# Weight subtractions of three attention stages on VectorE instead of GpSimd, and the value product emitted ahead of normalising q and k

## The chip, the cores and the metric

The kernel runs on one core of a Trainium2 chip. The metric is the time of one execution on the device, in microseconds (us); of several runs the median is taken.

A core has five engines, each with its own instruction queue that it works off in order: TensorE (PE, matrix products; PEld is its weight load), VectorE (DVE), ScalarE (ACT), GpSimd (POOL) and SyncE (SP), which issues the weight transfers here. An instruction that waits for another engine holds up all that stands behind it in its own queue.

## The reference

One sequence of 256 tokens with 1024 features goes through two transformer blocks of two layers with a mixture of experts, and then four layers with a plain MLP. The mixers, in order, are forgetting attention, latent attention, retention, block attention with a relative bias ("moba"), differential attention ("diff") and retention again. Cut to the two mixers that the change touches most:

```
# moba; 256 tokens are one block of 256, so every query sees its own causal block alone
q, k, v = split(h @ w_in, 3)                       # 16 heads of 64
q = rmsnorm(q, q_norm_w) * 64 ** -0.5;  k = rmsnorm(k, k_norm_w)
p = softmax(where(dist >= 0, q @ k.T + bias[bucket(dist)], -1e30))
out = (p @ v) @ w_out

# diff; 16 heads of q and k, 8 of v with 128 columns
p = softmax(as above).reshape(8 heads, 2, q, k)
o = (p[:, 0] - lambda * p[:, 1]) @ v
out = (rmsnorm(o, subln_w) * (1 - lambda_init)) @ w_out
```

Latent attention projects h to 768 columns for queries and a shared 256+32 for keys and values, and expands these per head; the rest of it is attention again.

## The kernel before

All weights are float32 in device memory. To multiply with them nearly exactly, the kernel makes two numbers of each: `wh`, the weight rounded to the engine's fast format, and `wl = raw - wh`, what the rounding lost. Activations are split in the same way (`hTh`, `hTl`; `aTh`, `aTl`). A product of such a pair is three matmuls: high by high, high by low, low by high (L169 to L171 in `tok_mm` with 256 columns each, and likewise in `feat_mm` and `acc_mm`).

`unit` (L137 to L156) brings in one weight block: SyncE starts the transfer into `raw`, ScalarE casts to `wh` (L147), and `wl` is made by one subtraction per piece of 128x1024 (or smaller) (L153). Which engine makes that subtraction is read from the table `SPL` by the name of the stage: with (1, 0) every subtraction of the stage is GpSimd's, with (2, 0) every second, and a stage that isn't in the table has them on VectorE. Before the change five stages are in it: forgetting attention (`fgt`), the two halves of latent attention (`latpre`, `latheads`), `moba` and `diff`. GpSimd makes 127 subtractions in all, 34 in `fgt`, 10 in `latpre`, 15 in `latheads`, 34 in `moba` and 34 in `diff`; VectorE makes 399 in the other stages and in half of `latheads`.

`_attn_layer` is the program of `moba` and of `diff`. It works on four groups of four heads. For a group, `proj` (L635 to L672) loads the weights of q, k and v (`uq`, `uk`, `uv`, two pieces each), multiplies h with q's and k's for both halves of the tokens (96 matmuls), squares the result on ScalarE (L647), adds it up by head on VectorE (L648, L652), takes the inverse root (`rsqrt`, L253 to L263, some twelve tiny VectorE operations on 128x16), scales q and k with it on VectorE (L659), transposes them on TensorE (L663) and copies them out on ScalarE. Only then comes the product with v's weights (L667 to L671, 48 matmuls). `mix` does the attention: scores on TensorE (L523), bias and row maximum on VectorE (L531), its sign (L533), exponential on ScalarE (L535), transposing the probabilities (L545) and the product with v. In `diff`, VectorE combines the two softmaxes (L690 to L693), and after the product ScalarE squares the result (L704), VectorE takes the inverse root again (L706, L253 to L263, here on 128x2 and 128x1) and scales (L710), and TensorE transposes the result (L210).

The order on each engine is set by a scheduler that goes by the order in which the code emits the work and by the engines' expected times, so work of the next group (its q and k products, tiles `pj__...`) is put between the dependent steps of the present one. `HOLD` sets from which subtraction on a stage's subtractions may not be placed ahead of a given point; it isn't changed.

Of the kernel before, what the change touches and what calls it, by code (L numbers as in the profile page):

```python
# [10 lines left out]
F32 = mybir.dt.float32  # L11
# [10 lines left out]
NT = S // 128  # L22
# [8 lines left out]
GU = 2  # L31
GE = 4
HOLD = dict(ret0=2, mlp0=2, mlp1=2, mlp2=2, mlp3=2, moba=4)
SPL = {'fgt': (1, 0), 'latpre': (1, 0), 'latheads': (2, 0), 'moba': (1, 0), 'diff': (1, 0)}
HL = 6
WX = 2
HOMES = "rhrhxhrhrhxhr"
# [47 lines left out]
class Net:  # L85
# [51 lines left out]
    def unit(self, ap, k, n):  # L137
# [4 lines left out]
        for k0 in range(0, k, step):  # L142
# [5 lines left out]
            self.nu += 1  # L148
            sh = SPL.get(self.ph, ())
            eng = nc.gpsimd if sh and self.nu % sh[0] in sh[1:] else nc.vector  # L150
# [462 lines left out]
    def _attn_layer(self, i, kind):  # L613
        nc, I = self.nc, self.I
        diff = kind == "diff"
        w, wo = I[kind + "_w_in_2"][0], I[kind + "_w_out_2"][0]
        gq = self.head_gain(I[kind + "_q_norm_2"][0], 0.125)
        gk = self.head_gain(I[kind + "_k_norm_2"][0], 1.0)
        if diff:
            init = 0.8 - 0.6 * math.exp(-0.3 * i)  # L620
            lb = self.bcast_row(I["diff_lambda_2"][0], 256, tag="lam")
            lv = lb.rearrange("p (a b d) -> p a b d", a=2, b=2)
            pr = self.wk.tile([128, 2, 64], F32, name="lpr", tag="lam")
            nc.vector.tensor_tensor(pr, lv[:, :, 0, :], lv[:, :, 1, :], OP.mult)
            l2 = self.sm.tile([128, 2], F32, name="l2", tag="l2")
            nc.vector.tensor_reduce(l2, pr, AX.X, OP.add)
            nc.scalar.activation(l2, l2, AF.Exp)
            nlam = self.sm.tile([128, 1], F32, name="nlam", tag="nlam")
            nc.vector.tensor_tensor(nlam, l2[:, 1:2], l2[:, 0:1], OP.subtract)
            nc.vector.tensor_scalar(nlam, nlam, -init, None, op0=OP.add)  # L630
            sub = self.bcast_row(I["diff_subln_2"][0], 128, tag="sub")
            nc.vector.tensor_scalar(sub, sub, 1.0 - init, None, op0=OP.mult)
        hT, r = self.prenorm(self.column("norm1_2", i * D))

        def proj(g):  # L635
            uq = self.unit(self.rows(w, 0, 8, g * 256, 256), 8, 256)
            uk = self.unit(self.rows(w, 0, 8, 1024 + g * 256, 256), 8, 256)
            uv = self.unit(self.rows(w, 0, 8, 2048 + g * 256, 256), 8, 256)
            bias = self.load_bias(g)
            ss = self.sm.tile([128, NT, 8], F32, name="qss", tag="qss")  # L640
            pss = []
            for tok in range(NT):
                ps = self.ppj()
                self.tok_mm(ps[:, 0:256], hT, tok, uq, 8, 0, True, True)
                self.tok_mm(ps[:, 256:512], hT, tok, uk, 8, 0, True, True)
                sq = self.wk.tile([128, 512], F32, name="sq", tag="sq")
                nc.scalar.activation(sq, ps, AF.Square, scale=r[:, tok:tok + 1])  # L647
                nc.vector.tensor_reduce(ss[:, tok, :], sq.rearrange("p (h d) -> p h d", d=64), AX.X, OP.add)  # L648
                qk = self.wk.tile([128, 512], F32, name="qk", tag="qk", bufs=4)
                nc.scalar.copy(qk, ps)  # L650
                pss.append(qk)
            nc.vector.tensor_scalar(ss, ss, 1.0 / 64, EPS, op0=OP.mult, op1=OP.add)  # L652
            rr = self.rsqrt(ss.rearrange("p t h -> p (t h)"), 16).rearrange("p (t h) -> p t h", t=NT)
            qT = self.wk.tile([128, 2, S], F32, name="qT", tag="qT", bufs=3)
            kT = self.wk.tile([128, 2, S], F32, name="kT", tag="kT", bufs=3)
            for tok in range(NT):
                nc.vector.tensor_scalar(rr[:, tok, :], rr[:, tok, :], r[:, tok:tok + 1], None, op0=OP.mult)
                qk = pss[tok].rearrange("p (h d) -> p h d", d=64)
                nc.vector.tensor_tensor(qk, qk, rr[:, tok, :, None].to_broadcast([128, 8, 64]), OP.mult)  # L659
                pt = self.pat()  # L660
                pv = pt.rearrange("p (k t) -> p k t", k=4)
                for m in range(4):
                    nc.tensor.transpose(pv[:, m, :], pss[tok][:, m * 128:m * 128 + 128], self.ident)  # L663
                t = slice(tok * 128, tok * 128 + 128)
                nc.scalar.mul(qT[:, :, t], pv[:, 0:2, :], gq)
                nc.scalar.mul(kT[:, :, t], pv[:, 2:4, :], gk)
            v = self.wk.tile([128, NT, 256], F32, name="v", tag="v", bufs=3)  # L667
            ps = self.ppj()
            for tok in range(NT):
                self.tok_mm(ps[:, tok * 256:tok * 256 + 256], hT, tok, uv, 8, 0, True, True)  # L670
                nc.scalar.mul(v[:, tok], ps[:, tok * 256:tok * 256 + 256], r[:, tok:tok + 1])  # L671
            return qT, kT, v, bias  # L672

        def mix(g, aT, qT, kT, v, bias):

            def q(h):
                return qT[h % 2 * 64:h % 2 * 64 + 64, h // 2, :]

            def k(h):
                return kT[h % 2 * 64:h % 2 * 64 + 64, h // 2, :]  # L680

            def bq(h, qb):
                return bias[:, h, 128 - qb * 128:256]

            for qb in range(NT):
                nb = qb + 1
                if diff:
                    o = self.wk.tile([128, 256], F32, name="o", tag="o")
                    p, rs = self.probs(q, k, bq, qb)
                    nc.vector.tensor_scalar(rs[:, :, 1], rs[:, :, 1], nlam, None, op0=OP.mult)  # L690
                    for m in range(2):
                        nc.vector.tensor_scalar(p[0][:, m, :], p[0][:, m, :], rs[:, m, 0:1], None, op0=OP.mult)
                        nc.vector.scalar_tensor_tensor(p[0][:, m, :], p[1][:, m, :], rs[:, m, 1:2], p[0][:, m, :],  # L693
                                                       op0=OP.mult, op1=OP.add)
                    pT = self.flip([p[0][:, m, kb * 128:kb * 128 + 128] for m in range(2) for kb in range(nb)])
                    po = self.pat()
                    for dh in range(2):
                        for kb in range(nb):
                            nc.tensor.matmul(po[:, dh * 128:dh * 128 + 128], pT[dh * nb + kb],
                                             v[:, kb, dh * 128:dh * 128 + 128], start=kb == 0, stop=kb == nb - 1)  # L700
                    ss = self.sm.tile([128, 2], F32, name="dss", tag="dss")
                    for dh in range(2):
                        junk = self.jk.tile([128, 512], F32, name="junk", tag="junk")
                        nc.scalar.activation(junk[:, :128], po[:, dh * 128:dh * 128 + 128], AF.Square,  # L704
                                             accum_out=ss[:, dh:dh + 1])
                    nc.vector.tensor_scalar(ss, ss, 1.0 / 128, EPS, op0=OP.mult, op1=OP.add)  # L706
                    rr = self.rsqrt(ss, 2)
                    for dh in range(2):
                        c = slice(dh * 128, dh * 128 + 128)
                        nc.vector.scalar_tensor_tensor(o[:, c], po[:, c], rr[:, dh:dh + 1], sub, op0=OP.mult,  # L710
                                                       op1=OP.mult)
                else:
                    o = self.attend(q, k, lambda kb, h: v[:, kb, h * 64:h * 64 + 64], bq, qb)
                self.to_T(o, aT, 2 * g, qb, n=2)

        self.heads(proj, mix, wo)


# [871 lines left out]
```

## Time and profile before

| | us |
|---|---|
| median of 3 runs | 2518.86 (2513.32 to 2525.78) |
| the profiled execution, its own time | 2524.33 |
| its span on the core | 2522.5 |
| stages: latent attention | 532.5 to 704 |
| moba | 1409 to 1574.3 |
| the MLP behind moba | 1575 to 1745 |
| diff | 1760.4 to 1936.3 |

The profile is that of one execution. TensorE is busy for 2276.9 us of the 2522.5 (90%), VectorE for 1310.5 (52%), ScalarE for 985.5 (39%) and GpSimd for 297.4 (12%). The granted clock is the share of its full speed at which TensorE ran in a stretch, 0.50 or 1.00. An engine's idle time before an instruction is put down to the instruction that it waited for; this is written as `<- DVE qk L659`. The stages are told apart by the names of the tiles (`at__moba__...`, `pj__diff__...`).

### The profile page before, as it was taken

Reading aid. Unit: us, or ns where it says so; the run is one execution under the profiler, and the core shown is the slowest. Engines: PE = TensorE matmul, PEld = TensorE weight load, DVE = VectorE, ACT = ScalarE, POOL = GpSimd, SP = SyncE. Lnnn points to the kernel's source line nnn. Section 1 sums busy time; section 2 is a strip of 40 time slices with the busy share of each in tenths; the row PEclk is TensorE's granted clock in tenths of the full one; section 3 lists DMA queues with packets and bytes.
Section 4 is the critical chain, followed back from the end, with each engine's and each line's share of the span. In section 5 each row is a group of like instructions: output and inputs, shape, how many; then the busy total and the mean of one; then the engine's idle time right before and its main releaser. Section 6 shows DMA issues by size and latency. Waiting matters only on the chain.

```text
span 2522.5 us, 34039 instructions
## 1 busy us (share of the span) xinstructions
PE 2276.9 (90%) x13606; PEld 1779.1 (71%) x13606; DVE 1310.5 (52%) x2465; ACT 985.5 (39%) x1622; POOL 297.4 (12%) x139
## 2 busy tenths in 40 slices
PE   4887999959989997979999888999678999999999
PEld 3787443348854333867899778998677998887997
DVE  7877110087840003645655544655667555665654
ACT  2444111146521112434444445444455444444443
POOL 2443000032200000000000443001441000000000
PEclk9888999979989998989999989999899999999999
DMA  9768999956689995554555423555423555544552
GB/s 302 244 206 290 348 365 395 354 191 206 228 306 400 397 387 212 165 169 150 167 191 191 158 79 117 170 198 169 135 87 125 190 185 182 176 151 155 177 191 84
DMA packets 310470, 541.96 MB, mean 215 GB/s; under 512 B 15752, under 2 KB 158720, under 8 KB 310304
## 3 DMA queue, kind: packets, MB, share of 16 engines
q1 hardware_dynamic: 298288, 528.84, 60.3%
q10 hardware_dynamic: 12016, 10.85, 1.4%
q8 instruction: 111, 1.82, 0.3%
q14 instruction: 55, 0.45, 0.1%
HBM read 538.57 MB, written 4.22 MB: 215 GB/s over the span
## 4 chain that ended last, share of the span: by engine, by line
PE 50%; DVE 7%; ACT 1%; issue 1%; ACTq 1%; DMA 0%
DVE rsa L259 1%; ACTq L588 1%; DVE wl L153 1%; DVE rsy L253 1%; DVE rsy L263 1%; DVE m L533 1%; DVE rsy L254 0%; DVE p L531 0%; PE acc__mlp__16304 L199 0%; PE acc__mlp__19715 L198 0%; PE acc__mlp__9577 L199 0%; PE acc__mlp__16302 L199 0%; PE acc__mlp__9576 L197 0%; PE acc__mlp__9575 L199 0%; PE acc__mlp__19713 L198 0%
## 5 line engine op out<-in xcount | busy, mean ns | idle before, releaser
L147 ACT CAST wh<-raw 128x1024 fp32r<-128x1024 f32 (+4 forms) x526 | 523.8, 1020 | 462.0 <-issue 71.8
L153 DVE TENSOR_TENSOR wl<-raw,wh 128x1024 fp32r<-128x1024 f32 (+1 forms) x399 | 476.4, 1215 | 380.7 <-ACT wh L147 378.0
L153 POOL TENSOR_TENSOR wl<-raw,wh 128x1024 fp32r<-128x1024 f32 (+4 forms) x127 | 287.3, 2280 | 1577.9 <-ACT wh L147 1570.3
L813 DVE SCALAR_TENSOR_TENSOR macc<-raw,c,macc 128x512 f32<-128x512 f32 x196 | 190.6, 973 | 5.6 <-DMA raw<-in_w_mod_dram 2.4
L535 ACT ACTIVATE p<-p,m 128x128 f32<-128x128 f32 (+1 forms) x128 | 57.0, 448 | 36.5 <-DVE m L533 36.3
L398 ACT CAST aTh<-rl 128x512 fp32r<-128x512 f32 x56 | 34.7, 620 | 78.4 <-DVE rl L396 78.4
L399 DVE TENSOR_TENSOR aTl<-rl,aTh 128x512 fp32r<-128x512 f32 x56 | 38.8, 693 | 38.5 <-ACT aTh L398 38.5
L276 ACT ACTIVATE junk<-x 128x512 f32<-128x512 f32 x52 | 32.7, 629 | 64.5 <-DVE x L341 33.3
L259 DVE SCALAR_TENSOR_TENSOR rsa<-rsy,rsh 128x1 f32<-128x1 f32 x186 | 50.4, 302 | 3.1
L396 DVE TENSOR_TENSOR rl<-rl 128x512 f32<-128x512 f32 x56 | 38.3, 685 | 0.0
L218 ACT CAST hTh<-xg 128x512 fp32r<-128x512 f32 (+1 forms) x36 | 21.2, 604 | 27.5 <-DVE xg L215 24.8
L219 DVE TENSOR_TENSOR hTl<-xg,hTh 128x512 fp32r<-128x512 f32 (+1 forms) x36 | 27.3, 777 | 2.4 <-ACT hTh L218 2.2
L533 DVE TENSOR_SCALAR m<-m 128x2 f32<-128x2 f32 x64 | 26.7, 418 | 0.5
L263 DVE SCALAR_TENSOR_TENSOR rsy<-rsa,rsy 128x2 f32<-128x2 f32 (+2 forms) x141 | 24.9, 177 | 3.9
L648 DVE TENSOR_REDUCE qss<-sq 128x8 f32<-128x512 f32 x16 | 10.9, 684 | 29.1 <-ACT sq L647 29.1
L535 ACT ACTIVATION_READ_ACCUMULATOR p<-p,m 128x1 f32 x128 | 24.1, 189 | 0.0
L1384 PE MATMUL acc__moe__2320<-dv,back 64*128 64x512 f32 x32 | 18.0, 641 | 2.7 <-ACT dv L1375 2.7
L1384 PE MATMUL acc__moe__6093<-dv,back 64*128 64x512 f32 x32 | 18.0, 641 | 2.5 <-ACT dv L1375 2.5
L1384 PE MATMUL acc__moe__2321<-dv,back 64*128 64x512 f32 x32 | 18.0, 641 | 0.0
L1384 PE MATMUL acc__moe__6094<-dv,back 64*128 64x512 f32 x32 | 18.0, 641 | 0.0
L824 PE MATMUL at__latpre__4036<-ones,macc 128*128 128x1 f32 x8 | 1.8, 351 | 16.6 <-DVEq L1231 16.6
L1384 PE MATMUL acc__moe__2323<-dv,back 64*128 64x512 f32 x32 | 16.8, 605 | 0.0
(3889 smaller groups left out, 7365.2 us busy)
## 6 DMA issues: line engine op xcount, KB each, us to landing
raw<-in_w_up_dram SPq DMA_DIRECT2D x64, 1024.0 KB, 5.5
raw<-in_w_down_dram SPq DMA_DIRECT2D x64, 1024.0 KB, 5.5
raw<-in_w_mod_dram SPq DMA_DIRECT2D x48, 1024.0 KB, 5.2
raw<-in_ret_w_in_dram SPq DMA_DIRECT2D x48, 1024.0 KB, 5.2
raw<-in_exp_w_gate_dram SPq DMA_DIRECT2D x40, 1024.0 KB, 12.4
raw<-in_exp_w_down_dram SPq DMA_DIRECT2D x34, 1024.0 KB, 13.0
raw<-in_exp_w_up_dram SPq DMA_DIRECT2D x30, 1024.0 KB, 11.3
wh<-in_exp_w_up_dram SPq DMA_DIRECT2D x34, 512.0 KB, 8.7
```

Of the source, the lines that this page charges most:

```text
L147: nc.scalar.copy(h[:, :m * n], p)
L153: eng.tensor_tensor(l[:, :m * n], p, h[:, :m * n].bitcast(F32), OP.subtract)
L259: nc.vector.scalar_tensor_tensor(a[:, c], y[:, c], h[:, c], y[:, c], op0=OP.mult, op1=OP.mult)
L263: nc.vector.scalar_tensor_tensor(y, a, 1.5, y, op0=OP.add, op1=OP.mult)
L276: nc.scalar.activation(junk[:, :w], p, AF.Square, scale=n ** -0.5, accum_out=ss[:, i, j:j + 1])
L396: nc.vector.tensor_tensor(rl, rl, rl, OP.mult)
L398: nc.scalar.copy(h, rl)
L399: nc.vector.tensor_tensor(aT[1][:, 2 * j:2 * j + 2, :].rearrange("p k t -> p (k t)"), rl, h.bitcast(F32), OP.subtract)
L533: nc.vector.tensor_scalar(mx, mx, -1.0, None, op0=OP.mult)
L535: nc.scalar.activation(p[:, m, :], p[:, m, :], AF.Exp, bias=mx[:, m:m + 1], accum_out=rs[:, m, s:s + 1])
L813: i = nc.vector.scalar_tensor_tensor(acc, r[:, k, :], self.c[:, kk:kk + 1], acc, op0=OP.mult, op1=OP.add)
L1384: mm(acc[tok][half], back[c, e % 4, tok * 128:tok * 128 + 128], dv[c, :], start=e == 0, stop=e == 15)
```

## The change

The table loses four of its five stages, so that 93 of GpSimd's 127 subtractions (10 and 15 of latent attention, 34 of moba, 34 of diff) become VectorE's. And in `proj` the product with v's weights is emitted right behind the sums of squares, ahead of the inverse root and of all that normalises and transposes q and k.

```diff
-SPL = {'fgt': (1, 0), 'latpre': (1, 0), 'latheads': (2, 0), 'moba': (1, 0), 'diff': (1, 0)}
+SPL = {'fgt': (1, 0)}
...
             nc.vector.tensor_scalar(ss, ss, 1.0 / 64, EPS, op0=OP.mult, op1=OP.add)
+            v = self.wk.tile([128, NT, 256], F32, name="v", tag="v", bufs=3)
+            ps = self.ppj()
+            for tok in range(NT):
+                self.tok_mm(ps[:, tok * 256:tok * 256 + 256], hT, tok, uv, 8, 0, True, True)
+                nc.scalar.mul(v[:, tok], ps[:, tok * 256:tok * 256 + 256], r[:, tok:tok + 1])
             rr = self.rsqrt(ss.rearrange("p t h -> p (t h)"), 16).rearrange("p (t h) -> p t h", t=NT)
...
                 nc.scalar.mul(kT[:, :, t], pv[:, 2:4, :], gk)
-            v = self.wk.tile([128, NT, 256], F32, name="v", tag="v", bufs=3)
-            ps = self.ppj()
-            for tok in range(NT):
-                self.tok_mm(ps[:, tok * 256:tok * 256 + 256], hT, tok, uv, 8, 0, True, True)
-                nc.scalar.mul(v[:, tok], ps[:, tok * 256:tok * 256 + 256], r[:, tok:tok + 1])
             return qT, kT, v, bias
```

Five lines are added ahead, so L657, L659 and L663 are L662, L664 and L668 afterwards.

TensorE in moba's second group, before, around the transposes of q and k. `pj__moba__11758` is the product with v's weights, and `qk` is what VectorE has normalised (L659). Between the last matmul with q's and k's weights and the first row of L663 stand 24 matmuls of v, 5 of the next group (`pj__moba__11935`) and 9 more of v.

```order
L171 MATMUL pj__moba__11758<-wh,hTl 128x256
L663 MATMUL at__moba__11741<-ident,qk 128x128 x4
L169 MATMUL pj__moba__11758<-wh,hTh 128x256
L663 MATMUL at__moba__11750<-ident,qk 128x128 x4
L170 MATMUL pj__moba__11758<-wl,hTh 128x256
```

The same place after the change; v's product is now `pj__moba__11723`.

```order
L170 MATMUL pj__moba__11723<-wl,hTh 128x256
L171 MATMUL pj__moba__11723<-wh,hTl 128x256
L668 MATMUL at__moba__11793<-ident,qk 128x128 x4
L668 MATMUL at__moba__11802<-ident,qk 128x128 x4
L171 MATMUL pj__moba__11935<-wh,hTl 128x256
```

All 48 matmuls of v and 5 of the next group, 53 where there were 38, now stand between the products of q and k and their transposes, and what follows the transposes belongs to the next group. In moba's first group the count goes from 44 to 54, in diff's first from 44 to 70.

VectorE in moba's second group, before: the inverse root of the sums of squares (`qss`), which ends in L659 a few rows on.

```order
L253 TENSOR_SCALAR rsy<-qss 128x16
L255 TENSOR_SCALAR rsh<-qss 128x16
L254 TENSOR_SCALAR rsy<-rsy 128x16
L261 TENSOR_TENSOR rsa<-rsy 128x16
L262 TENSOR_TENSOR rsa<-rsa,rsh 128x16
L263 SCALAR_TENSOR_TENSOR rsy<-rsa,rsy 128x16
```

The same rows after.

```order
L253 TENSOR_SCALAR rsy<-qss 128x16
L255 TENSOR_SCALAR rsh<-qss 128x16
L254 TENSOR_SCALAR rsy<-rsy 128x16
L261 TENSOR_TENSOR rsa<-rsy 128x16
L153 TENSOR_TENSOR wl<-raw,wh 128x1024
L262 TENSOR_TENSOR rsa<-rsa,rsh 128x16
L263 SCALAR_TENSOR_TENSOR rsy<-rsa,rsy 128x16
```

One subtraction (L153) now stands in this chain, between two steps of the inverse root; two more stand right behind the chain, ahead of the first L531.

VectorE in diff's first group, before: the inverse root of the sums of squares of the first result (`dss`). L259 and L263 come twice more and L710 then makes `o`, which TensorE transposes in L210.

```order
L253 TENSOR_SCALAR rsy<-dss 128x2
L255 TENSOR_SCALAR rsh<-dss 128x2
L693 SCALAR_TENSOR_TENSOR p<-p,rs 128x256
L254 TENSOR_SCALAR rsy<-rsy 128x2
L648 TENSOR_REDUCE qss<-sq 128x8
L259 SCALAR_TENSOR_TENSOR rsa<-rsy,rsh 128x1 x2
L263 SCALAR_TENSOR_TENSOR rsy<-rsa,rsy 128x2
```

A piece of the same chain after, from the second L259 to the third.

```order
L652 TENSOR_SCALAR qss<-qss 128x16
L153 TENSOR_TENSOR wl<-raw,wh 128x1024
L263 SCALAR_TENSOR_TENSOR rsy<-rsa,rsy 128x2
L253 TENSOR_SCALAR rsy<-qss 128x16
L255 TENSOR_SCALAR rsh<-qss 128x16
L259 SCALAR_TENSOR_TENSOR rsa<-rsy,rsh 128x1 x2
L254 TENSOR_SCALAR rsy<-rsy 128x16
```

The second half of the tokens' inverse root for the next group's q and k (`qss`) and a subtraction now stand between two steps of the first result's chain; from its first L253 to its L710 there are four subtractions, where there was none. On TensorE 83 matmuls stand between that result's product (L699) and its transposes (L210), where there were 41.

## Rows read from the trace of the kernel before

**Rows 1.** Windows by stage: busy us (instructions) of PE, PEld, DVE, ACT, POOL; clock; DMA.

```profile
532.50:704.00 171.50, 151.97 (x963) 138.24 (x964) 140.31 (x335) 96.72 (x217) 42.91 (x21) 0.91 0.65 219
1409.00:1574.30 165.30, 136.97 (x1019) 128.13 (x1018) 85.39 (x212) 83.32 (x171) 70.85 (x32) 0.93 0.36 115
1575.00:1745.00 170.00, 168.34 (x1104) 153.83 (x1103) 98.42 (x115) 78.91 (x97) 0.00 (x0) 1.00 0.57 186
1760.40:1936.30 175.90, 131.21 (x947) 123.46 (x946) 120.11 (x370) 84.01 (x199) 70.82 (x32) 0.89 0.34 109
```

**Rows 2.** Timeline, moba's first group, GpSimd: start, duration, instruction [idle before <- releaser].

```profile
1424.18 11.76 POOL L153 TENSOR_TENSOR wl<-raw,wh 128x1024 fp32r<-128x1024 f32 x5 [5.53 <-ACT wh L147]
```

**Rows 3.** Timeline of VectorE beside it.

```profile
1429.04 2.32 DVE L253 TENSOR_SCALAR rsy<-qss 128x16 int32<-128x16 int32 x1
...
1433.59 2.38 DVE L254 TENSOR_SCALAR rsy<-rsy 128x16 int32<-128x16 int32 x1
```

**Rows 4.** Timeline of TensorE beside it.

```profile
1431.64 0.28 PE L170 MATMUL pj__moba__11436<-wl,hTh 128*128 128x256 f32 x1
1431.76 0.28 PE L171 MATMUL pj__moba__11436<-wh,hTl 128*128 128x256 f32 x1
1438.91 1.11 PE L663 MATMUL at__moba__11419<-ident,qk 128*128 128x128 f32 x4 [6.87 <-DVE qk L659]
```

**Rows 5.** Waits of TensorE in moba: total us, times, longest.

```profile
PE at__moba__11419 L663 <- DVE qk L659: 6.9, 1, 6.9
...
PE at__moba__12385 L663 <- DVE qk L659: 2.6, 1, 2.6
PE at__moba__11832 L545 <- ACT p L535: 2.3, 2, 1.4
...
PE at__moba__12476 L545 <- ACT p L535: 1.3, 1, 1.3
```

**Rows 6.** Timeline, diff's first group, VectorE.

```profile
1809.92 0.16 DVE L253 TENSOR_SCALAR rsy<-dss 128x2 int32<-128x2 int32 x1
...
1812.46 2.51 DVE L259 SCALAR_TENSOR_TENSOR rsa<-rsy,rsh 128x1 f32<-128x1 f32 x2
1815.01 2.26 DVE L263 SCALAR_TENSOR_TENSOR rsy<-rsa,rsy 128x2 f32<-128x2 f32 x1
```

**Rows 7.** Timeline of GpSimd beside it.

```profile
1812.59 4.66 POOL L153 TENSOR_TENSOR wl<-raw,wh 128x1024 fp32r<-128x1024 f32 x2 [11.14 <-ACT wh L147]
```

**Rows 8.** Waits of TensorE in diff.

```profile
PE at__diff__15921 L210 <- DVE o L710: 7.0, 1, 7.0
PE at__diff__14711 L663 <- DVE qk L659: 6.3, 1, 6.3
...
PE at__diff__14838 L210 <- DVE o L710: 4.3, 1, 4.3
...
PE at__diff__14807 L545 <- DVE p L693: 2.8, 1, 2.8
PE at__diff__14906 L210 <- DVE o L710: 2.7, 1, 2.7
...
PE at__diff__15168 L545 <- DVE p L693: 1.4, 1, 1.4
```

**Rows 9.** Lines of VectorE in diff: busy us, mean ns of one.

```profile
L259 DVE SCALAR_TENSOR_TENSOR rsa<-rsy,rsh 128x1 f32<-128x1 f32 x54 | 21.2, 433 | 0.9
L533 DVE TENSOR_SCALAR m<-m 128x2 f32<-128x2 f32 x16 | 8.6, 538 | 0.1
```

**Rows 10.** Lines by form, the MLP behind moba: VectorE's subtraction.

```profile
L153 DVE TENSOR_TENSOR wl<-raw,wh 128x1024 fp32r<-128x1024 f32 x60 | 71.9, 1223 | 59.4 <-ACT wh L147 59.2
```

**Rows 11.** The subtraction's line on VectorE, whole kernel: its idle time before it.

```profile
  ACT wh L147: 378.0, 194
```

**Rows 12.** Waits of TensorE in latent attention.

```profile
PE pj__latpre__4322 L171 <- DVE h2l L869: 10.1, 2, 7.9
```

**Rows 13.** Timeline of VectorE ahead of that wait's end.

```profile
561.94 4.43 DVE L259 SCALAR_TENSOR_TENSOR rsa<-rsy,rsh 128x1 f32<-128x1 f32 x2
```

## The prediction

> **What bounds the kernel now.** I read the windows by stage first, then TensorE's waits in the stages that the change touches, then the timelines around the longest of them. TensorE sets the time: in the MLP behind moba it is busy for 168.34 of 170 us, at clock 1.00, while VectorE makes all 60 subtractions and GpSimd does nothing [rows 1, 10]. In moba TensorE is busy for 136.97 of 165.3 us at clock 0.93, in diff for 131.21 of 175.9 at 0.89, in latent attention for 151.97 of 171.5 at 0.91; these are three of the stages in which GpSimd works [rows 1]. So what can be won is TensorE's idle time there (28.3, 44.7 and 19.5 us) and part of what the lower clock cost. The mean of 0.93 in moba, with only 0.50 and 1.00 granted, is 0.14 of the stage at half clock, 23 us, and 0.22 of diff, 39 us; were TensorE busy all through these, it would have lost half of each, so 11.6 and 19.3 us are the upper bounds of the clock's cost.
>
> Who is waited for: in moba VectorE's normalised q and k, one wait in each of four groups (6.9, 4.5, 4.4, 2.6 us, 18.4 in all), then the softmax (four waits, 2.3 down to 1.3, 6.8 in all) [rows 5]. In diff it is VectorE's L710, five waits of 7.0 down to 2.7 (23.5 in all), once q and k (6.3), and the softmaxes' combination (four, 2.8 down to 1.4, 8.6 in all) [rows 8].
>
> Why VectorE is late, although it is busy for only 85 of moba's 165 us: in moba's first group GpSimd runs five subtractions from 1424.18 on without a break [rows 2]. In just this stretch three VectorE instructions on 128x16 stand one behind the other, the first of 2.32 us, the last of 2.38 [rows 3]. L253 on 128x2 lasts 0.16 with GpSimd idle, and when GpSimd begins in diff at 1812.59, a pair of L259 lasts 2.51 and L263 2.26 [rows 6, 7]. So a small VectorE operation that falls into a GpSimd subtraction (11.76 / 5 = 2.35 us each, [rows 2]) lasts about until that ends. Three such in a row are 7.1 us for half a microsecond of work, and TensorE's wait in that place is 6.87 [rows 4].
>
> **The change part by part.** *Subtractions moved.* On GpSimd a 128x1024 piece takes 2.35 us, on VectorE 1.22 [rows 2, 10]. Moba and diff have 34 each, so VectorE gets at most 34 x 1.22 = 41.5 us more in each stage, and loses what it was held up. In diff, L259 takes 433 ns in the mean of 54 and L533 538 of 16 [rows 9]; at some 0.17 each that is 14.2 and 5.9 us of hold-up in these two lines alone.
>
> *Moba, q and k.* The order shows 15 more matmuls ahead of the transposes in three groups and 10 more in the first; matmuls of this size start 0.12 us apart [rows 4], so the cover grows by 1.8 us (1.2 in the first). One subtraction, 1.22 us, now stands in the chain. Taking the hold-ups away is worth about the whole wait in the first group (7.1 less 0.5 against 6.9), and I take it as worth most of the smaller ones. I leave about 0.7 us a group: 18.4 - 2.9 = 15.5 us won. Bounds: 7 (cover alone, 1.2 + 3 x 1.8) and 18.4.
>
> *Moba, softmax.* Ahead of the exponential stand L531 and L533 on VectorE, L533 held up as well (538 ns in the mean in diff [rows 9]); but two subtractions now stand right ahead of L531 in a group (2.4 us), which start early as long as their casts are there. I take half of 6.8 away, 3.5; bounds -3 and 6.8.
>
> *Moba, clock.* Fewer gaps, less time at half clock: 5 us of the 11.6, bounds 0 and 11.6. Moba in sum: 15.5 + 3.5 + 5 = 24; bounds 4 and 37.
>
> *Diff, L710.* Four subtractions (4.9 us) and part of the next group's inverse root now stand inside the chain, which held about 4.3 us of hold-up in the place shown [rows 6]. So the chain gets a little longer, and what decides is the cover: 83 matmuls instead of 41 ahead of the transposes, 42 x 0.12 = 5.0 us. The wait there, 4.3 us [rows 8], would shrink to about that of 4.3 - 4.3 + 4.9 - 5.0, near nothing; I leave 1.5 us in each of five: 23.5 - 7.5 = 16. Bounds: 0 (the cover is taken from the next wait) and 23.5.
>
> *Diff, the rest.* The first group's q and k get 26 more matmuls, 3.1 us, and lose their hold-ups: 5 of 6.3. The combination of the softmaxes: 2 of 8.6, since subtractions stand around it too. Clock: 4 of 19.3, the gaps being only partly closed. Against it, 3 us for casts: where VectorE makes the subtractions, it sat idle for 378.0 us in 194 waits for `wh`, 1.95 us each [rows 11], and in an in-order queue the chain behind waits too. Diff in sum: 16 + 5 + 2 + 4 - 3 = 24; bounds 0 and 45 (all of its idle time).
>
> *Latent attention.* TensorE waits 10.1 us for L869 [rows 12], and shortly ahead of that a pair of L259 lasts 4.43 us [rows 13]. VectorE is busy for 140 of 171 us there, and gets 25 subtractions, some of them in front of L869. I take 6 us, bounds -5 and 15. GpSimd's own pace was no bound anywhere: it is busy for 71 of 165 us.
>
> **A rule weighed.** The rows say that VectorE's idle half is enough for the subtractions in moba. In diff VectorE is busy for 120.11 of 175.9 us; without the 20 us of hold-up found and with 41.5 more it is at 141 of an expected 152. The Trainium skill (Perfetto Trace Analysis, Optimizing Scalar/DVE Operations) has it that, where VectorE is saturated, some of its work may well go to ScalarE or even to GpSimd; it adds that the two share a read port, so that moving work between them might not help. By the first half diff's subtractions were better left where they are; by the second, which the long small operations bear out, they were not.
>
> **The rivals.** *A: VectorE becomes the pace in diff.* For: 141 of 152 us, in a stage in which chains alternate with ScalarE and TensorE, and four subtractions in each L710 chain. Against: the cover of 42 more matmuls. If diff wins nothing, 24 fall away: 2465 + 24 = 2489.
>
> *B: the change doesn't do what it says*, the small operations being slow for another reason. Then only the cover counts: 6.6 in moba, and in diff 3.1 and at best 5.0 for each of five waits, while some five subtractions a group in chains cost 1 x 1.22 x 4 and 4 x 1.22 x 4, 24 us. 6.6 + 3.1 + 17 (cover up to the waits that are there) - 24 is 3 us won: 2516. Against it: each of the long operations lies inside GpSimd's stretch, and equal ones outside don't last [rows 2, 3, 6, 7].
>
> *C: slower.* VectorE works its queue in order. If all 68 subtractions of moba and diff came to stand in chains that TensorE waits for, they would cost 68 x 1.22 = 83 us, against 64 us of waits in these chains today (18.4 + 6.8 + 23.5 + 6.3 + 8.6, all gone at best): 19 us slower, 2538. It decides from 52 of the 68 on. Against it: the order puts one a group into moba's chain and four or five into diff's, 22 or so of 68; the others stand where VectorE would idle. With the casts' waits of 1.95 us exposed in each of these 22 (43 us more) it could still come out.
>
> **How the numbers follow.** The sum is made against the profiled execution: 2524.33 - 24 - 24 - 6 = 2470.3. That execution is 5.5 us above the median of 2518.86; taken from the median it is 2464.9, and that is predicted, 2465. Forecast 0.66; A 0.21; B 0.07; C 0.06. The terms' bounds together give 2421 (all at their best) and 2520 (all at their worst). Both at once are unlikely; two thirds of the way to the best, and half of that from A to the worst, give 2436 to 2504, which leaves out B, C and some of either tail. A measurement of this kernel can tell about 0.5% from no change, 12.6 us, so faster means under 2506 and slower over 2531: forecast and A, 0.87; B is within, 0.07; C slower, 0.06.
>
> **What would show it.** In the profile of the changed kernel GpSimd has only forgetting attention's subtractions and a few others; the 2.3 us operations of VectorE in moba and diff are gone (L253 and L533 at some 0.17 us). TensorE's waits for q and k in moba fall to 3 us in all, and moba's stage to about 141 us, diff's to about 152 at a clock of 0.9 or more, with VectorE near 0.93 of it; latent attention to about 165. A is right if diff keeps over 40 us of TensorE's idle time, with subtractions in front of L710 in VectorE's timeline; C if moba too waits behind `wl <- wh`. The forecast is wrong if VectorE waits for casts inside the chains, or if the operations stay long.

## The result, and the profile after

| | us |
|---|---|
| before, median | 2521.63 (2513.32 to 2525.78) |
| after, median | 2445.63 (2441.74 to 2449.13) |
| ratio | 0.9702, 95% interval 0.9672 to 0.9733 |
| the profiled execution after, its own time | 2445.27 (span 2443.5) |

The change makes the kernel 76 us faster, 3.0%; 2465 was forecast, with 2436 to 2504 as the range. The stages are cut out of the two traces as in the table of before, from a stage's first matmul to its last (us):

| | forgetting | latent | moba | diff |
|---|---|---|---|---|
| before | 188.3 | 171.5 | 165.3 | 175.9 |
| after | 186.1 | 160.4 | 140.1 | 134.1 |
| won | 2.2 | 11.1 | 25.2 | 41.8 |
| forecast | | 6 | 24 | 24 |

The four won sum to 80.3 us; the two profiled executions differ by 79.1, so all that lies outside these stages changed by about 1 us in sum. Moba is as forecast, diff won nearly twice as much.

The windows of the three stages after (columns as in [rows 1], latent attention first):

```profile
528.90:689.30 160.40, 149.55 (x963) 137.22 (x964) 132.33 (x357) 95.96 (x217) 0.00 (x0) 0.92 0.67 223
1396.00:1536.10 140.10, 131.63 (x1019) 121.53 (x1018) 87.58 (x244) 82.72 (x171) 0.00 (x0) 0.99 0.41 129
1723.70:1857.80 134.10, 123.73 (x947) 114.29 (x946) 108.79 (x401) 82.16 (x200) 0.00 (x0) 0.97 0.45 143
```

Two differences to [rows 1] tell where the gain comes from. A stage less TensorE's busy time is its idle time: 28.3 to 8.5 us in moba, 44.7 to 10.4 in diff. And TensorE's busy time itself fell, for the same 1019 and 947 matmuls, by 5.3 and 7.5 us, while the mean granted clock rose from 0.93 to 0.99 and from 0.89 to 0.97; these are put down to the clock here. Idle time and clock together are the whole gain: 19.8 + 5.3 = 25.1, 34.3 + 7.5 = 41.8. VectorE is a surprise: it got some 32 subtractions more in each of the two stages, of nearly 1.2 us each, and its busy time went from 85.39 to 87.58 in moba and from 120.11 down to 108.79 in diff. What it had been busy with was waiting.

VectorE's timeline in moba's first group after, in the place of [rows 3]: the inverse root that is one chain.

```profile
1416.92 0.17 DVE L253 TENSOR_SCALAR rsy<-qss 128x16 int32<-128x16 int32 x1
1417.01 0.17 DVE L255 TENSOR_SCALAR rsh<-qss 128x16 f32<-128x16 f32 x1
1417.13 0.18 DVE L254 TENSOR_SCALAR rsy<-rsy 128x16 int32<-128x16 int32 x1
```

The same three instructions that lasted 2.3 to 2.4 us each last 0.17. What TensorE still waits for, first q and k in moba, then the longest in diff (in the place of [rows 5, 8]):

```profile
PE at__moba__11471 L668 <- DVE qk L664: 0.2, 1, 0.2
```

```profile
PE at__diff__15989 L210 <- DVE o L710: 2.6, 1, 2.6
...
PE at__diff__15890 L545 <- DVE p L693: 1.6, 1, 1.6
...
PE at__diff__15628 L210 <- DVE o L710: 0.7, 1, 0.7
...
PE at__diff__14763 L668 <- DVE qk L664: 0.2, 1, 0.2
```

In moba 18.4 us of waits for q and k became 0.2. In diff the 23.5 us for L710 became 3.3, the 6.3 for q and k 0.2.

### The profile page after: what moved, and what is told of

The parts are those of the page before. It is cut to its first block, busy times and chain, and to the rows that moved or that the text cites. A ratio compares the mean times of both kernels' runs of the same rounds, so it can differ in the third digit from the quotient of the medians.

```text
span 2443.5 us, 33945 instructions
## 1 busy us (share of the span) xinstructions
PE 2263.2 (93%) x13606; PEld 1762.4 (72%) x13606; DVE 1297.5 (53%) x2558; ACT 982.3 (40%) x1622; POOL 93.8 (4%) x46
## 4 chain that ended last, share of the span: by engine, by line
PE 52%; DVE 5%; ACT 1%; ACTq 1%; issue 1%; DMA 0%; DVEq 0%
DVE wl L153 2%; ACTq L588 1%; ACT wh L147 1%; DVE rsa L259 0%; DVE rsy L263 0%; DVE og L502 0%; PE acc__mlp__19713 L197 0%; PE acc__mlp__16304 L199 0%; PE acc__mlp__16303 L197 0%; PE acc__mlp__9577 L199 0%; PE acc__mlp__12855 L198 0%; PE acc__mlp__9575 L199 0%; PE acc__mlp__19714 L199 0%; PE acc__mlp__16302 L199 0%; PE acc__mlp__19714 L197 0%
## 5 line engine op out<-in xcount | busy, mean ns | idle before, releaser
L153 DVE TENSOR_TENSOR wl<-raw,wh 128x1024 fp32r<-128x1024 f32 (+2 forms) x492 | 575.8, 1189 | 393.4 <-ACT wh L147 387.6
L813 DVE SCALAR_TENSOR_TENSOR macc<-raw,c,macc 128x512 f32<-128x512 f32 x196 | 176.5, 901 | 4.9 <-DMA raw<-in_w_mod_dram 2.1
L153 POOL TENSOR_TENSOR wl<-raw,wh 128x1024 fp32r<-128x1024 f32 (+1 forms) x34 | 83.7, 2482 | 134.4 <-ACT wh L147 121.5
L259 DVE SCALAR_TENSOR_TENSOR rsa<-rsy,rsh 128x1 f32<-128x1 f32 x186 | 34.4, 216 | 2.6
L1170 POOL TENSOR_TENSOR hTl<-xg,hTh 128x512 fp32r<-128x512 f32 x8 | 9.9, 1266 | 475.2 <-DVE top L1193 455.5
L263 DVE SCALAR_TENSOR_TENSOR rsy<-rsa,rsy 128x2 f32<-128x2 f32 (+2 forms) x141 | 22.6, 161 | 3.2
L535 ACT ACTIVATION_READ_ACCUMULATOR p<-p,m 128x1 f32 x128 | 24.1, 188 | 0.0
L219 DVE TENSOR_TENSOR hTl<-xg,hTh 128x512 fp32r<-128x512 f32 (+1 forms) x36 | 23.5, 671 | 0.9 <-ACT hTh L218 0.7
L1384 PE MATMUL acc__moe__2320<-dv,back 64*128 64x512 f32 x32 | 18.0, 641 | 2.7 <-ACT dv L1375 2.7
L1384 PE MATMUL acc__moe__6093<-dv,back 64*128 64x512 f32 x32 | 18.0, 641 | 2.7 <-ACT dv L1375 2.7
L1384 PE MATMUL acc__moe__6094<-dv,back 64*128 64x512 f32 x32 | 18.0, 641 | 0.0
L1384 PE MATMUL acc__moe__2321<-dv,back 64*128 64x512 f32 x32 | 18.0, 641 | 0.0
L1384 PE MATMUL acc__moe__6096<-dv,back 64*128 64x512 f32 x32 | 16.9, 608 | 0.0
L811 DVE TENSOR_SCALAR macc<-raw,c 128x512 f32<-128x512 f32 x28 | 15.5, 553 | 2.5 <-DMA raw<-in_w_mod_dram 2.5
L1384 PE MATMUL acc__moe__2323<-dv,back 64*128 64x512 f32 x32 | 16.8, 605 | 0.0
## 6 DMA issues: line engine op xcount, KB each, us to landing
raw<-in_exp_w_up_dram SPq DMA_DIRECT2D x30, 1024.0 KB, 10.1
```

The source lines that it names most:

```text
L153: eng.tensor_tensor(l[:, :m * n], p, h[:, :m * n].bitcast(F32), OP.subtract)
L219: nc.vector.tensor_tensor(lo[:, k0:k0 + n, tok * 128:tok * 128 + 128], pv, d.bitcast(F32), OP.subtract)
L259: nc.vector.scalar_tensor_tensor(a[:, c], y[:, c], h[:, c], y[:, c], op0=OP.mult, op1=OP.mult)
L535: nc.scalar.activation(p[:, m, :], p[:, m, :], AF.Exp, bias=mx[:, m:m + 1], accum_out=rs[:, m, s:s + 1])
L813: i = nc.vector.scalar_tensor_tensor(acc, r[:, k, :], self.c[:, kk:kk + 1], acc, op0=OP.mult, op1=OP.add)
L1384: mm(acc[tok][half], back[c, e % 4, tok * 128:tok * 128 + 128], dv[c, :], start=e == 0, stop=e == 15)
```

## The experiments

Two theories stood against each other. H: a GpSimd subtraction holds up VectorE's small operations while it runs, and TensorE waits for VectorE; the move of the subtractions is the gain. C: the value product, now ahead of the transposes, covers VectorE's chains; the move of the product is the gain. All ratios are to the kernel before, timed beside each.

### One part without the other

The subtractions moved, the value product left in its place:

```diff
-SPL = {'fgt': (1, 0), 'latpre': (1, 0), 'latheads': (2, 0), 'moba': (1, 0), 'diff': (1, 0)}
+SPL = {'fgt': (1, 0)}
```

> The subtractions of latent, moba and diff attention on VectorE, the value product left where it was. Theory H (GpSimd's subtractions hold up VectorE's small operations, and that was the loss): nearly all of the gain stays, 2455 to 2465 us, with VectorE's L253 and L533 at some 0.17 us in moba and diff. Theory C (the gain is the value product's cover ahead of the transposes): only latent attention's 11 us and a little more are won, 2500 us or above. If the two parts need one another, TensorE waits for q and k in moba 2 to 4 us a group.

2445.61 us, ratio 0.9694 (0.9653 to 0.9734): all of the gain, and 10 us below the best that H had expected. Moba takes 142.1 us, diff 136.8. No wait of TensorE for q and k or for L710 is above 2.6 us, so the moved subtractions don't need the moved product.

The value product moved, the table left as it was:

```diff
             nc.vector.tensor_scalar(ss, ss, 1.0 / 64, EPS, op0=OP.mult, op1=OP.add)
+            v = self.wk.tile([128, NT, 256], F32, name="v", tag="v", bufs=3)
...
             rr = self.rsqrt(ss.rearrange("p t h -> p (t h)"), 16).rearrange("p (t h) -> p t h", t=NT)
...
```

> The value product moved, the subtractions left on GpSimd. Theory H: the long VectorE operations stay at 2.3 us, moba and diff win only the cover of 1.2 to 1.8 us a group in moba and some in diff, 2505 to 2515 us. Theory C: 2460 to 2470 us.

2524.19 us, ratio 1.0006 (0.9988 to 1.0025): nothing. C is out, and H's own expectation of some 10 us of cover missed too. TensorE's waits in moba show why, and the timelines of GpSimd, VectorE and TensorE in its first group:

```profile
PE at__moba__11471 L668 <- DVE qk L664: 7.9, 1, 7.9
PE at__moba__12115 L668 <- DVE qk L664: 7.0, 1, 7.0
PE at__moba__11793 L668 <- DVE qk L664: 6.3, 1, 6.3
PE at__moba__12437 L668 <- DVE qk L664: 4.0, 1, 4.0
```

```profile
1422.24 14.09 POOL L153 TENSOR_TENSOR wl<-raw,wh 128x1024 fp32r<-128x1024 f32 x6 [5.54 <-ACT wh L147]
```

```profile
1425.35 0.69 DVE L648 TENSOR_REDUCE qss<-sq 128x8 f32<-128x512 f32 x1 [3.89 <-ACT sq L647]
...
1427.09 2.32 DVE L253 TENSOR_SCALAR rsy<-qss 128x16 int32<-128x16 int32 x1
1429.33 2.43 DVE L255 TENSOR_SCALAR rsh<-qss 128x16 f32<-128x16 f32 x1
1431.67 2.39 DVE L254 TENSOR_SCALAR rsy<-rsy 128x16 int32<-128x16 int32 x1
1434.10 2.26 DVE L261 TENSOR_TENSOR rsa<-rsy 128x16 f32<-128x16 f32 x1
```

```profile
1439.08 1.11 PE L668 MATMUL at__moba__11471<-ident,qk 128*128 128x128 f32 x4 [7.91 <-DVE qk L664]
```

There are 9 to 15 matmuls more ahead of the transposes, and the waits for them grew, from 18.4 to 25.2 us. GpSimd now runs six subtractions without a break where it ran five [rows 2], and a fourth VectorE operation falls into them; in each of the other three groups four long operations stand in the chain where there were two. Reckon in each group from the start of the last L648 to the transposes, and sum over the four: TensorE had matmuls to do for 16.8 us of this stretch before and 23.3 now, so the cover came, 6.5 us of it. But the chain itself went from 35.2 to 48.5 us, 13.3 longer, and the waits grew by the difference. What the cover won, more hold-ups took. Diff takes 180.8 us against 175.9, at clock 0.86 against 0.89; this profiled execution, of 2532.38 us, was the longest of ten, so part of that is scatter.

### GpSimd idling along

The changed kernel, with a subtraction on GpSimd that nobody reads beside each one that VectorE makes in moba and diff:

```diff
                 eng.tensor_tensor(l[:, :m * n], p, h[:, :m * n].bitcast(F32), OP.subtract)
+            if self.ph in ("moba", "diff"):
+                g = self.wk.tile([128, self.part], F32, name="ballast", tag="ballast", bufs=1)
+                nc.gpsimd.tensor_tensor(g[:, :m * n], h[:, :m * n].bitcast(F32), h[:, :m * n].bitcast(F32), OP.subtract)
```

> The changed kernel, and for each subtraction that VectorE makes in moba and diff GpSimd makes one of its own of the same size into a scratch tile, wh minus wh, whose result nobody reads; every other engine has the same instructions in the same order as in the changed kernel. Theory H: VectorE's operations are held up again, now its subtractions too, moba and diff lose 15 to 35 us each, 2480 to 2510 us. If order and engine of the subtraction alone made the gain: 2445 to 2450 us. It computes the same result.

2536.02 us, ratio 1.0051 (1.0034 to 1.0067): 90 us slower than the changed kernel and slower than the kernel before. Moba and diff take 183.7 us each. This is the strongest of the runs for H, since the instructions of all other engines and their order are those of the changed kernel, and no instruction in the trace waits for one of the ballast's. VectorE in moba, its chain and then a pair of its own subtractions, and GpSimd beside it:

```profile
1421.31 2.32 DVE L153 TENSOR_TENSOR wl<-raw,wh 128x1024 fp32r<-128x1024 f32 x1
1423.55 1.86 DVE L655 TENSOR_SCALAR qss<-qss 128x16 f32<-128x16 f32 x1
...
1425.53 1.87 DVE L258 TENSOR_SCALAR rsh<-qss 128x16 f32<-128x16 f32 x1
...
1432.56 2.35 DVE L153 TENSOR_TENSOR wl<-raw,wh 128x1024 fp32r<-128x1024 f32 x2
```

```profile
1416.96 12.38 POOL L156 TENSOR_TENSOR ballast<-wh 128x1024 f32<-128x1024 f32 x5
```

Up to 1429.3 GpSimd runs; until then a subtraction on VectorE lasts 2.32 us and an operation on 128x16 up to 1.87. Behind that, two subtractions last 2.35 together. The expectation was 15 to 35 us a stage and 2510 at most; it was 43.6 in moba and 49.6 in diff. That VectorE's own subtractions would be held up was part of the expectation, but priced too low: VectorE's busy time rose by 41 us in each of the two stages, from 87.58 to 128.56 and from 108.79 to 150.10.

GpSimd with a copy in place of the subtraction:

```diff
-                nc.gpsimd.tensor_tensor(g[:, :m * n], h[:, :m * n].bitcast(F32), h[:, :m * n].bitcast(F32), OP.subtract)
+                nc.gpsimd.tensor_copy(g[:, :m * n], h[:, :m * n].bitcast(F32))
```

> As the run with idle GpSimd subtractions, but GpSimd copies wh into the scratch tile (one tensor read in place of two). If what holds VectorE is that GpSimd runs at all, for as long as it runs: the loss shrinks in proportion to the copy's duration; at an estimated 1.2 us (half of 2.4) about 45 us of the 90, 2490 us. If it is the second read alone: 2445 to 2450 us. It computes the same result.

2482.02 us, ratio 0.9842 (0.981 to 0.9875). The copy of 128x1024 takes 1.53 us in the mean against 2.42, and costs 36 us against 90: moba 12.1 instead of 43.6, diff 24.1 instead of 49.6. So a single read holds VectorE up too, and the loss falls faster than the duration.

### By the instruction, or by the time that both run?

The kernel before, each of GpSimd's subtractions cut into instructions of 256 columns:

```diff
-                eng.tensor_tensor(l[:, :m * n], p, h[:, :m * n].bitcast(F32), OP.subtract)
+                if eng is nc.gpsimd:
+                    for i0 in range(0, m * n, 256):
+                        i1 = min(i0 + 256, m * n)
+                        eng.tensor_tensor(l[:, i0:i1], p[:, i0:i1], h[:, i0:i1].bitcast(F32), OP.subtract)
+                else:
+                    eng.tensor_tensor(l[:, :m * n], p, h[:, :m * n].bitcast(F32), OP.subtract)
```

> The kernel before, with each of GpSimd's subtractions cut into instructions of 256 columns (a 128x1024 piece is four); who makes what stays. If a small VectorE operation is held until the GpSimd instruction that runs ends (theory H, held by the instruction): the long operations in moba and diff fall from 2.3 us to at most some 0.7 each, about half of the 60 us of these stages comes back, 2485 to 2505 us. If GpSimd's work as such slows VectorE, in proportion to the time that both run (theory S): the sum of the hold-ups stays, 2520 us or more, the cut's own cost added.

2483.86 us, ratio 0.9848 (0.9824 to 0.9872). The time met H's expectation, but not where H put it: forgetting attention wins 20.6 us, diff 10.4, moba only 3.4 (the profiled execution took 2491.41 us, 7.5 above the median). VectorE and GpSimd in moba's first group:

```profile
1407.63 0.65 DVE L258 TENSOR_SCALAR rsy<-qss 128x16 int32<-128x16 int32 x1
1408.20 0.78 DVE L260 TENSOR_SCALAR rsh<-qss 128x16 f32<-128x16 f32 x1
1408.90 0.78 DVE L259 TENSOR_SCALAR rsy<-rsy 128x16 int32<-128x16 int32 x1
1409.71 0.67 DVE L266 TENSOR_TENSOR rsa<-rsy 128x16 f32<-128x16 f32 x1
...
1415.18 0.65 DVE L268 SCALAR_TENSOR_TENSOR rsy<-rsa,rsy 128x16 f32<-128x16 f32 x1
```

```profile
1404.02 13.81 POOL L156 TENSOR_TENSOR wl<-raw,wh 128x256 fp32r<-128x256 f32 x20 [3.08 <-ACT wh L147]
```

A piece lasts 13.81 / 20 = 0.69 us, and for as long as GpSimd has a next one, every VectorE operation of the chain lasts about one piece: one for one, twelve in a row. So the hold is by the instruction, until the running one ends. By its time alone moba would fit theory S as well, since nearly all of its loss stayed; the single operations decide against S. Shorter instructions did little for this chain of twelve steps: it took 8.2 us from L258 to the last L268, in the kernel before three long operations and nine short ones made it about 9. They did more where VectorE's own operations are longer: in forgetting attention the 84 sums of the modulation last 0.93 us in the mean, against 1.15 in the kernel before.

### Is VectorE the pace in diff?

```diff
-SPL = {'fgt': (1, 0)}
+SPL = {'fgt': (1, 0), 'diff': (2, 0)}
```

> The changed kernel with every second subtraction of diff on GpSimd. Rival A (VectorE is the pace in diff, so part of its work is better left to GpSimd): diff at 130 us or less, 2435 to 2442 us. Theory H: 17 GpSimd subtractions bring hold-ups of up to 2.3 us back, diff 12 to 25 us longer, 2457 to 2470 us.

2465.22 us, ratio 0.9771 (0.9746 to 0.9796), and diff takes 152.5 us against 134.1. Giving back half of the subtractions costs 18 us: rival A is out. VectorE was busy for 108.79 of 134.1 us with all of them, and is for 118.76 of 152.5 with half.

### What the subtractions cost on VectorE, and what the order gives

The value product late, no subtraction of latent attention on GpSimd, and in moba and diff no subtraction at all; the matmuls read `wh` in place of `wl` there, as many as before:

```diff
-SPL = {'fgt': (1, 0), 'latpre': (1, 0), 'latheads': (2, 0), 'moba': (1, 0), 'diff': (1, 0)}
+SPL = {'fgt': (1, 0)}
...
-            with self.tc.issue_after(self.last) if self.last and self.nsplit > HOLD.get(self.ph, 99) else nullcontext():
-                eng.tensor_tensor(l[:, :m * n], p, h[:, :m * n].bitcast(F32), OP.subtract)
+            if self.ph in ("moba", "diff"):
+                l = h
+            else:
+                with self.tc.issue_after(self.last) if self.last and self.nsplit > HOLD.get(self.ph, 99) else nullcontext():
+                    eng.tensor_tensor(l[:, :m * n], p, h[:, :m * n].bitcast(F32), OP.subtract)
```

> The run with the subtractions on VectorE and the value product left where it was, but in moba and diff the subtraction isn't made at all (left out: the matmuls read wh in place of wl there, as many as before). The scheduler then plans no work on VectorE for it, and TensorE's order is that of the kernel before again: 41, 32, 37, 28, 37, 28, 40, 28 matmuls in diff between a result's product and its transposes, where it is 83, 46, 50, 45, 61, 43, 67, 9 with the subtractions on VectorE. If the hold-ups alone were the loss: moba and diff within 6 us of the run with the subtractions (142.1 and 136.8 us), 2435 to 2448 us, so the 68 subtractions cost next to nothing on VectorE. If the cover that the new order gives is needed for it, as the prediction had it: L710 is still waited for by some 2 to 4 us in most of eight places, diff 145 to 155 us, 2450 to 2465 us.

2429.15 us, ratio 0.9636 (0.9613 to 0.9659); moba 131.6 us, diff 126.3. The two longest of TensorE's waits for L710 (L713 here) in diff:

```profile
PE at__diff__15931 L213 <- DVE o L713: 0.5, 1, 0.5
...
PE at__diff__14866 L213 <- DVE o L713: 0.4, 1, 0.4
```

With the cover of before, L710 is waited for by half a microsecond at the most. So without the hold-ups the old order was enough, and both expectations of this run were off: the stages are not within 6 us of the run with the table alone changed (142.1 and 136.8 us), but 10.5 below it in each. This splits the gain: taking GpSimd's subtractions away is worth 33.7 us in moba and 49.6 in diff, and making them on VectorE gives 10.5 back in each. The longer cover serves to pay for these. It came with the table: the scheduler plans the subtractions as VectorE's work, and puts the same 83 matmuls in diff's first place whether the product moves or not.

### Further on the same way

Forgetting attention's subtractions on VectorE too:

```diff
-SPL = {'fgt': (1, 0)}
+SPL = {}
```

> The changed kernel with forgetting attention's 34 subtractions on VectorE as well, so GpSimd has none. Theory H by itself: that stage too loses its hold-ups, up to 8 us faster, 2437 us. Against it: VectorE is busy for 7 to 8 tenths of that stage's time with the modulation's sums, so the subtractions could stand in TensorE's way there, up to 6 us slower, 2452 us.

2419.76 us, ratio 0.9593 (0.9552 to 0.9634): 26 us better than the changed kernel. Forgetting attention takes 161.0 us against 186.1. The sums of the modulation there, by form, in the kernel before and in this one:

```profile
L813 DVE SCALAR_TENSOR_TENSOR macc<-raw,c,macc 128x512 f32<-128x512 f32 x84 | 96.9, 1154 | 1.6
```

```profile
L813 DVE SCALAR_TENSOR_TENSOR macc<-raw,c,macc 128x512 f32<-128x512 f32 x84 | 61.7, 744 | 0.5
L153 DVE TENSOR_TENSOR wl<-raw,wh 128x1024 fp32r<-128x1024 f32 x30 | 36.3, 1219 | 2.6 <-ACT wh L147 2.5
```

The 84 sums are 35.2 us shorter, about what the 30 subtractions add; VectorE's busy time fell from 152.89 us to 137.71. Up to 8 us had been expected.

The same with the value product late:

```diff
-SPL = {'fgt': (1, 0), 'latpre': (1, 0), 'latheads': (2, 0), 'moba': (1, 0), 'diff': (1, 0)}
+SPL = {}
```

> No subtraction on GpSimd, forgetting attention's neither, and the value product left where it was before. Against the same with the product moved (2419.8 us): if moving it is worth nothing once the hold-ups are gone, 2417 to 2424 us; if its cover is worth the 1.2 to 1.8 us a group that the order shows, 2426 to 2436 us.

2422.11 us, ratio 0.9599 (0.9574 to 0.9624). The two intervals overlap widely: where the product stands makes no difference that these runs can tell.

And the last arithmetic of GpSimd, the activation subtractions of the expert layers, on top of the empty table:

```diff
-SPL = {'fgt': (1, 0)}
+SPL = {}
...
-                    nc.gpsimd.tensor_tensor(hl[:, tok, c], xn, hh[:, tok, c].bitcast(F32), OP.subtract)
+                    nc.vector.tensor_tensor(hl[:, tok, c], xn, hh[:, tok, c].bitcast(F32), OP.subtract)
```

> As the run with no weight subtraction on GpSimd (2419.8 us), and the four activation subtractions of each of the two expert layers on VectorE too, so GpSimd does no arithmetic at all. Hold-up theory: each of these eight lasts 1.26 us on GpSimd beside the routing's small VectorE operations, up to 1 us each won, 2412 to 2418 us. Against it: on VectorE they stand in the routing's chain at some 0.7 us each, 0 to 5 us lost, 2420 to 2425 us.

2406.17 us, ratio 0.955 (0.9528 to 0.9572): the best of all, 39 us below the changed kernel. The eight operations take 0.68 us each on VectorE against 1.27 on GpSimd, and the run is 13.6 us below the one with them on GpSimd, measured in another session; the intervals of the two ratios just meet (0.9552 to 0.9572). That is more than the hold-ups of eight operations of 1.27 us could be worth. The first expert layer with what follows it up to latent attention takes 293.2 us against 297.9, the second, up to retention, 289.4 against 296.3. What else was waiting for GpSimd there wasn't looked into.

## Why the prediction was right, and where not

*The cause.* TensorE's waits for VectorE, and VectorE held up by GpSimd, were read right: with GpSimd's subtractions back as ballast all is lost again, with them gone in any way it is won. Rivals B and C are out by the trace after; C's 83 us of subtractions in chains cost 21. B's price had a slip: five waits covered by at most 5.0 us each are 20.6 us by [rows 8] and not 17, so B stood at 2512 rather than 2516.

*Moba, 24 forecast, 25.2 measured.* Waits for q and k 18.2 won (15.5 forecast), the softmax 5.9 of 6.8 (3.5), the clock 5.3 (5). The end of the stage gave back some 5 us in new waits of at most 0.9 each, for `wl` and for L341, which had no term. So it is partly luck that the sum came out: two terms were some 5 us too low together, and the missing one took as much away.

*Diff, 24 forecast, 41.8 measured.* This is where the sum was too small, and the terms that were mis-sized are these: L710 won 20.2 us (16), q and k 6.1 (5), the combination of the softmaxes 6.0 (2), the clock 7.5 (4), and the 3 us set against it for casts weren't there: no wait of TensorE in diff ends on a weight's cast. The step in which the chain with four subtractions in it would be as long as the chain with its hold-ups was right to the microsecond in the place shown. Before, it runs from 1809.45 to 1817.91; after:

```profile
1760.27 0.17 DVE L706 TENSOR_SCALAR dss<-dss 128x2 f32<-128x2 f32 x1 [0.37 <-ACT junk L704]
...
1766.94 1.22 DVE L153 TENSOR_TENSOR wl<-raw,wh 128x1024 fp32r<-128x1024 f32 x1
...
1768.27 0.61 DVE L710 SCALAR_TENSOR_TENSOR o<-at__diff__14812,rsy,gb 128x128 f32<-128x128 f32 x2
```

That is 8.6 us against 8.5, and the 42 matmuls of cover made the wait vanish. What was wrong is the 1.5 us left in each of five places; 3.3 us are left in all.

*VectorE's load.* It was put at 141 us of an expected 152 in diff, and came to 108.79 of 134.1. The hold-up was found in two lines and taken as 20 us; it was twice that. In the run with no subtraction in moba and diff, VectorE does the rest of its work there with GpSimd idle (moba first):

```profile
1397.30:1528.90 131.60, 127.87 (x1019) 119.95 (x1018) 54.15 (x213) 82.00 (x171) 0.00 (x0) 1.00 0.46 145
1715.00:1841.30 126.30, 119.29 (x947) 111.26 (x946) 80.47 (x369) 83.14 (x199) 0.00 (x0) 1.00 0.48 152
```

So of diff's 120.11 us 39.6 were hold-up, and of moba's 85.39 it was 31.2. And in diff the subtractions added 28.3 us of busy time, 108.79 less 80.47, not 41.5. Rival A rested on these two terms.

*Latent attention, 6 forecast, 11.1 measured.* The wait for L869 went from 10.1 to one of 5.6 for `wl`; the per-head half of the stage won 8, for which the sum had nothing.

*The value product.* Its cover was counted as won in moba (bound 7 us, cover alone). By itself it comes, 6.5 us, and is lost to a chain that got 13.3 us longer; with the hold-ups gone these runs show nothing left for it to cover.

## What to carry to other kernels

An engine's busy time can be waiting: compare one instruction's duration beside another engine's work with its duration alone before you call an engine slow or full. Work moved to an idle engine isn't free if that engine shuts out a busy one; here moving some 32 subtractions of up to 1.22 us per stage onto the busier engine lowered its busy time in one stage and hardly raised it in the other. And once the hold-ups are gone, look for the next place of the same kind, since taking from GpSimd what the change had left it was worth another 39 us. Of these, 26 go with the shorter sums of forgetting attention; for the rest, in the expert layers, the cause stays open.

## What the runs showed of the hardware

Not every VectorE operation is held up by GpSimd. In the kernel before, GpSimd runs from 1475.40 to 1480.06 in moba, and VectorE beside it:

```profile
1476.13 0.29 DVE L531 CUSTOM_DVE_ANT_0 p<-sc__moba__11810,bias 128x128 f32<-128x128 f32 x1 [4.26 <-PE sc__moba__11811 L523]
...
1476.77 1.00 DVE L533 TENSOR_SCALAR m<-m 128x2 f32<-128x2 f32 x1
1477.69 0.28 DVE L531 CUSTOM_DVE_ANT_0 p<-sc__moba__11811,bias 128x128 f32<-128x128 f32 x1
...
1478.01 2.08 DVE L533 TENSOR_SCALAR m<-m 128x2 f32<-128x2 f32 x1
```

L531 reads scores from PSUM, and lasts 0.28 us as it does alone; L533 works on two numbers per partition in SBUF, and waits for the GpSimd instruction to end. So does a sum of two SBUF tensors (L813: 0.74 us in the mean with no GpSimd subtraction in the stage, 1.15 with them). The reduction of one SBUF tensor (L648) isn't held up inside the stretch of [rows 2], and lasts 0.68 to 0.69 us in the changed kernel too:

```profile
1427.30 0.69 DVE L648 TENSOR_REDUCE qss<-sq 128x8 f32<-128x512 f32 x1 [3.90 <-ACT sq L647]
```

The hold goes both ways. In the run with the ballast a GpSimd subtraction takes 1.89 us at its shortest (at 1448.45, for one). Here both engines start one in the same moment, VectorE's takes its usual time, and GpSimd's takes 1.1 us longer:

```profile
1776.97 1.21 DVE L153 TENSOR_TENSOR wl<-raw,wh 128x1024 fp32r<-128x1024 f32 x1
```

```profile
1776.97 2.96 POOL L156 TENSOR_TENSOR ballast<-wh 128x1024 f32<-128x1024 f32 x1 [1.59 <-ACT wh L147]
```

The Trainium skill (SBUF — State Buffer, SBUF: two separate sides) has the rule: VectorE and GpSimd share a pair of ports, which one of them holds for a whole instruction while the other is fully blocked, and VectorE needs it for operations that use two ports or have two SBUF inputs. The runs agree: 2.3 us beside 2.35 us instructions, 0.65 beside pieces of 0.69, nothing for reads of PSUM. Which of VectorE's operations on one SBUF input use two ports isn't to be seen in a trace; here L253 and L533 were held up and L648 was not.
